# A decoder step on one Trainium2 core: the last projection and norm with tokens on partitions

## The chip, the cores and the metric

The kernel runs on one core of a Trainium2 chip. The metric is device time in microseconds for one execution, the median of three runs. Five engines work side by side: TensorE (PE; its weight loads stand in the trace as PEld), VectorE (DVE), ScalarE (ACT), GpSimd (POOL) and SyncE (SP), which here issues all transfers. Each engine works its own instructions in order and waits for the others through semaphores.

## The reference

One step of a two-layer decoder of width 1024 on 264 tokens: a prompt of 256 and eight sample tokens. Layer 0 mixes with a gated short convolution, layer 1 with attention (eight heads of 128). Each layer ends alike, and the end of layer 1 is what matters here:

```python
z = x1 @ w_z                                   # the last quarter of layer 1's input projection
y = (o.reshape(B, T, 1024) * silu(z)) @ w_out  # o: attention output
x = ALPHA * x1 + y                             # ALPHA = sqrt(2)
mu, var = x.mean(-1), square(x - mu).mean(-1)
out = (x - mu) * rsqrt(var + 1e-5) * g + b
```

## The kernel before

**Layout.** Everything is kept feature-major: `xf` holds the residual as 128 partitions x 8 feature blocks x 264 tokens (`N`; the last eight are the samples). A weight matrix is cut into slabs of 128 output features (8 blocks of 128 x 128); 80 slabs are worked in order. Slabs 40 to 71 are layer 1's input projection (q, k, v, z; `S` = 40), 72 to 79 its output projection.

**Precision.** A product is done as three fp32r matmuls: high part of the weight with high and low part of the activation, low part of the weight with the high part (`mm`, lines 121 to 128). The high part of a slab is a ScalarE cast (`hi`, line 114), the low part a VectorE subtraction (`lo`, line 119). A slab's weight is the stationary operand, the 264 tokens move past it. `m0h`, `m0l` and `m1h`, `m1l` are the activation pairs; the gated attention output `g` of the last projection is the pair `m0`.

**Order.** There is no loop scheduler. `at(n, phase, f)` (line 134) hangs a call on slab `n`, `begin(n)` runs the hooks of a slab in a fixed order of phases ahead of its matmuls, and each engine takes them in that order. Splits of slab n stand at slab n - 5 (`hi`) and one behind (`lo`), with exceptions (`hi_slot`, `lo_slot`). `load` (line 101) uses four raw buffers: the load of a slab is issued by SyncE once the low part of the slab four before has been taken. High and low parts have six buffers each. Cache pages (32 loads) share ten buffers of the pool `kvp`.

**Slabs 64 to 71.** For head `f`, `z_evac` (line 778) takes silu of the accumulator and multiplies by the attention output in `qh`; `g_split` (791) makes the pair. The samples' attention ends in between: `pvd` (741) at slab 67, `od_copy` (754) at 68, transposes on TensorE (`od_tr`, 758) and `os_fin` (763) at 69. Samples of the first six heads are multiplied in a batch (`g_batch`, 796); the last two go through `z_evac`. The earlier score products of the cache keys (`qk`, line 690 on, matmul at 697) use four column groups of TensorE with 16 columns of weight each.

**The last projection and norm, lines 925 to 964.** `out_slabs` (337) runs slabs 72 to 79 with 24 matmuls of 264 columns each; eight further ones subtract the mean of block 0 (`shift`, 269). Behind each slab come the residual (`evac`, 262), squares on ScalarE (282) and sums on GpSimd (289, 290). After slab 79 four short groups of matmuls sum over partitions (298), the statistics are finished (308 to 312), and mean and inverse are broadcast to all partitions by matmuls (`bcast_one`, 332), with three matmuls that only keep TensorE busy between them (933). Then come a subtraction (946), a multiplication (936) and an affine pass (941, 943) for each of eight blocks, shared between VectorE, GpSimd and ScalarE, and four stores of two blocks (964).

Of the kernel before, what the change touches and what calls it, by code (L numbers as in the profile page):

```python
# [10 lines left out]
F32 = mybir.dt.float32  # L11
# [7 lines left out]
D = 1024  # L19
# [10 lines left out]
EARLY = (40, 41, 42)  # L30
NU = 7
# [4 lines left out]
C_ST = 56  # L36
# [11 lines left out]
def build(tc, a):  # L48
# [3 lines left out]
    with ExitStack() as top:  # L52
# [200 lines left out]
        class Norm:  # L253
# [75 lines left out]
            def bcast_one(self, nm, c):  # L329
                p = att_tile(f"lnb{c}")[:, 0:N]  # L330
                for j in range(4):
                    pe.matmul(p[:, G * j:G * j + G], sel[:, j], self.st[:, G * c:G * c + G],  # L332
                              start=True, stop=True)
                t = self.t(nm)
                act.copy(t, p)
                return p, t

# [174 lines left out]
        with tc.tile_pool(name="l1", bufs=1) as p1, ExitStack() as late_pool:  # L512
# [5 lines left out]
            kh = [p1.tile([128, N], F32, name=f"k{h}") for h in range(8)]  # L518
# [255 lines left out]
            late = {"n": 0}  # L774

            g_t = {}

            def z_evac(f, acc):
                z = p1.tile([128, N], F32, tag="z", bufs=2, name="z")
                act.activation(z, acc, AF.Silu)  # L780
                if late["n"]:
                    n_ = N
                    pool.tensor_copy(qh[f][:, T:N], os_[:, f])
                else:
                    n_ = T
                    pool.tensor_copy(zs[:, f], z[:, T:N])
                gt = p2.tile([128, N], F32, tag="rp", bufs=3, name="gt")
                g_t[f] = gt[:, 0:n_]
                dve.tensor_mul(gt[:, 0:n_], z[:, 0:n_], qh[f][:, 0:n_])  # L789

            def g_split(f):
                n_ = g_t[f].shape[-1]
                act.copy(g[0][:, f, 0:n_], g_t[f])
                dve.tensor_sub(g[1][:, f, 0:n_], g_t[f], g[0].bitcast(F32)[:, f, 0:n_])

            def g_batch(nf):
                gt = p2.tile([128, 8, 8], F32, name="gtb")
                dve.tensor_mul(gt[:, 0:nf], os_[:, 0:nf], zs[:, 0:nf])
# [231 lines left out]
```

## Time and profile before

| | |
|---|---|
| median of three runs | 287.8 us (287.7 to 287.8) |
| the profiled execution | 287.21 us |
| its span in the trace | 285.4 us |
| TensorE busy | 275.6 us, 97% |
| VectorE, ScalarE, GpSimd busy | 186.7, 160.2, 81.5 us |
| first matmul of slab 72 | 249.03 us |
| start of the last projection matmul | 273.06 us |

Times in the trace count from the span's start. A line number with an L names the line of the kernel that made the instruction. Matmuls are pipelined: a row's duration includes its way through the array, so the distance between two starts tells what one costs. A merged row (x3) covers several instructions from the first start to the last end. In the chain that ended last, each step starts where the one that released it ended.

### The profile page before, as it was taken

To read this page: it belongs to the slowest core of one execution; us is meant where nothing else is said; L and a number is where in the kernel's file an instruction comes from. 1 tells how busy PE (TensorE), PEld (TensorE's weight loads), DVE (VectorE), ACT (ScalarE), POOL (GpSimd) and SP (SyncE) were. 2 spreads that over 40 slices of the span, in tenths; PEclk is the share of its full clock that TensorE was granted. 3 is DMA by queue.
4 is the path that set the end of the run, shared out by engine and by line. 5 is a ranking of instruction groups with operands and counts; after the bars stand their busy time and mean duration, and the time that the engine had idled before them with its cause. 6 is when DMAs were issued, how large, how long until landed. Compare 5 with 4: busy or idle time off the path is not lost.

```text
span 285.4 us, 6265 instructions
## 1 busy us (share of the span) xinstructions
PE 275.6 (97%) x2345; PEld 261.8 (92%) x2345; DVE 186.7 (65%) x350; ACT 160.2 (56%) x307; POOL 81.5 (29%) x151
## 2 busy tenths in 40 slices
PE   8999999999999999999999999999999999999980
PEld 4999999999999999999979997999869969999960
DVE  2978866556758758858997683888545355646144
ACT  4876554445556546544976683568638634562123
POOL 3222322021010106919631087201100001206643
PEclk9999999999999999999999999999999999999995
DMA  7986889999675764413039998988929972410004
GB/s 225 412 286 212 258 293 333 379 369 370 232 255 182 254 230 152 148 46 106 0 119 293 408 398 311 351 294 282 297 79 294 376 271 76 153 69 1 2 0 153
DMA packets 22640, 64.02 MB, mean 224 GB/s; under 512 B 2770, under 2 KB 5202, under 8 KB 22610
## 3 DMA queue, kind: packets, MB, share of 16 engines
q1 hardware_dynamic: 22610, 63.63, 63.9%
q8 instruction: 18, 0.29, 0.4%
q14 instruction: 12, 0.10, 0.1%
HBM read 60.30 MB, written 3.32 MB: 223 GB/s over the span
## 4 chain that ended last, share of the span: by engine, by line
PE 94%; DMA 2%; DVE 1%; ACT 1%; SPq 0%; issue 0%; DVEq 0%; ACTq 0%
PE acc L126 26%; PE acc L128 26%; PE acc L127 26%; PE sd L697 3%; PE dps L749 3%; DMA first<-first 2%; PE acc L451 1%; PE s L630 1%; PE o L669 1%; PE acc L452 1%; PE acc L455 1%; PE pt L660 1%; PE s L629 1%; DVE xf L936 1%; PE lnb L332 1%; PE o L670 1%
## 5 line engine op out<-in xcount | busy, mean ns | idle before, releaser
L119 DVE TENSOR_TENSOR lo<-raw,hi 128x1024 fp32r<-128x1024 f32 x76 | 94.3, 1250 | 5.1 <-ACT hi L114 4.9
L114 ACT CAST hi<-raw 128x1024 fp32r<-128x1024 f32 x76 | 79.2, 1049 | 32.8 <-DMA raw<-w 18.9
L128 PE MATMUL acc<-m0h,lo 128*128 128x264 f32 (+1 forms) x344 | 97.5, 283 | 0.0
L126 PE MATMUL acc<-m0h,hi 128*128 128x264 f32 (+1 forms) x344 | 97.4, 283 | 0.0
L127 PE MATMUL acc<-m0l,hi 128*128 128x264 f32 (+1 forms) x344 | 97.4, 283 | 0.0
L126 PE MATMUL acc<-m1h,hi 128*128 128x264 f32 x264 | 76.7, 290 | 0.0
L128 PE MATMUL acc<-m1h,lo 128*128 128x264 f32 x264 | 74.8, 283 | 0.0
L127 PE MATMUL acc<-m1l,hi 128*128 128x264 f32 x264 | 74.6, 283 | 0.0
L128 PEld LDWEIGHTS acc<-m0h,lo 128*128 128x128 f32 x344 | 64.9, 189 | 0.0
L126 PEld LDWEIGHTS acc<-m0h,hi 128*128 128x128 f32 x344 | 64.8, 188 | 0.1
L127 PEld LDWEIGHTS acc<-m0l,hi 128*128 128x128 f32 x344 | 64.7, 188 | 0.0
L126 PEld LDWEIGHTS acc<-m1h,hi 128*128 128x128 f32 x264 | 49.7, 188 | 1.7 <-issue 1.7
L127 PEld LDWEIGHTS acc<-m1l,hi 128*128 128x128 f32 x264 | 49.7, 188 | 0.1
L128 PEld LDWEIGHTS acc<-m1h,lo 128*128 128x128 f32 x264 | 49.7, 188 | 0.0
L407 POOL COPY uo<-up 128x10 f32<-128x10 f32 x8 | 9.0, 1126 | 65.6 <-DVE up L406 59.5
L282 ACT ACTIVATE sqm<-xf 128x264 f32<-128x264 f32 x14 | 5.8, 422 | 20.1 <-DVE xf L262 20.1
L262 DVE SCALAR_TENSOR_TENSOR xf<-xf,acc 128x264 f32<-128x264 f32 x16 | 6.6, 424 | 12.5 <-PE acc L269 10.6
L638 DVE TENSOR_TENSOR s<-s,cst 128x256 f32<-128x256 f32 x8 | 3.4, 430 | 15.5 <-PE s L630 15.5
L290 POOL TENSOR_TENSOR q<-q,sqm 128x264 f32<-128x264 f32 x12 | 13.1, 1089 | 1.6 <-ACT sqm L282 1.5
L789 DVE TENSOR_TENSOR gt<-z,q 128x256 f32<-128x256 f32 (+1 forms) x8 | 3.4, 428 | 13.0 <-ACT z L780 13.0
L609 POOL COPY vs<-vh 128x8 f32<-128x8 f32 x8 | 1.6, 204 | 35.0 <-ACT vh L608 35.0
L289 POOL TENSOR_TENSOR sr<-sr,xf 128x264 f32<-128x264 f32 x10 | 9.3, 928 | 2.3 <-DVE xf L262 2.3
(176 smaller groups left out, 358.6 us busy)
## 6 DMA issues: line engine op xcount, KB each, us to landing
raw<-w SPq DMA_DIRECT2D x76, 512.0 KB, 4.6
kv<-kc SPq DMA_DIRECT2D x32, 256.0 KB, 5.9
kv<-vc SPq DMA_DIRECT2D x16, 512.0 KB, 5.7
first<-first SPq DMA_DIRECT2D x7, 388.0 KB, 6.3
k_o<-k SPq DMA_DIRECT2D x8, 132.0 KB, 5.1
v_o<-vh SPq DMA_DIRECT2D x8, 132.0 KB, 4.2
y_o<-xf SPq DMA_DIRECT2D x4, 264.0 KB, 2.6
cst<-cst SPq DMA_DIRECT2D x1, 392.0 KB, 6.3
```

The costliest lines, as they stand in the source:

```text
L114: act.copy(his[n][sl], raws[n][sl])
L119: dve.tensor_sub(los[n][sl], raws[n][sl], his[n].bitcast(F32)[sl])
L126: pe.matmul(acc, wh, mh[:, k, 0:w], start=first and k == ks[0], stop=False)
L127: pe.matmul(acc, wh, ml[:, k, 0:w], start=False, stop=False)
L128: pe.matmul(acc, wl, mh[:, k, 0:w], start=False, stop=last and k == ks[-1])
L262: dve.scalar_tensor_tensor(x, x, ALPHA, acc, ALU.mult, ALU.add)
L282: act.activation(self.last_sq, xf[:, m], AF.Square)
L289: pool.tensor_tensor(self.sr, self.sr, xf[:, m], ALU.add)
L290: pool.tensor_tensor(self.q, self.q, self.last_sq, ALU.add)
L407: pool.tensor_copy(uo[:, f], up[:, T:N + 2])
L697: pe.matmul(s[32 * j:32 * j + 16, 0:256], zq[:, o:o + 16], kt, start=step == 0 and i == 0, stop=step == 3 and i == 3)
L749: pe.matmul(dps[0][32 * j:32 * j + 32, 512 * c:512 * c + 512], pm[b2][pg][:, j, :], kv_tiles[step, j][:, 512 * c:512 * c + 512], start=ste ...
```

## The change

The last projection turns its operands round. Columns of the gated activation (128 tokens) become the stationary operand and the output weight moves, 512 or 256 columns at a time, so that the result has tokens on partitions and features along the row; the norm is then taken along the row by VectorE's statistics instruction, with no matmul and no broadcast.

- The weight of slabs 72 to 79 is stored by rows instead of by output blocks; slab 72 + k is input block k, with all 1024 outputs. Tokens 0 to 127 come first, over all eight slabs, then the samples, then tokens 128 to 255 in pieces of 512, 256 and 256 columns. The first half still runs through `begin`, so the hooks of slabs 72 to 79 now fall between its steps.
- `x1` has to be turned as well. VectorE transposes 32 x 32 blocks of `xf` into `kall` (the former key tiles, now one tile) at slabs 65 to 67; 16 transfers at slabs 68 to 71 move the blocks back into `xf` with tokens on partitions. The order of the outputs that results (`turned`) is put into the weight, the gains and biases, and taken back by the host.
- The samples leave the fp32r path: `gs` is multiplied in fp32 with the raw weight, eight tokens padded to 32, on four column groups; four small transfers bring the result from four groups of partitions into rows.
- Gains and biases are loaded as 2 x 128 x 1024 values (`gb_load`, slab 73). Raw slabs 76 to 79 and the parts of 78 and 79 live in the cache pool.
- Of tokens 128 to 255, columns 0 to 191 are finished by ScalarE and GpSimd (`other_way`), the rest by VectorE; three stores end the kernel.

The diff, cut:

```diff
+LATE = (78, 79)
...
+        def acc_full():
+            return psp.tile([128, 512], F32, tag="acc", bufs=3, name="acc")
         def acc_tile():
-            return psp.tile([128, 512], F32, tag="acc", bufs=3, name="acc")[:, 0:N + 2]
+            return acc_full()[:, 0:N + 2]
...
         def load(n):
-            raws[n] = wp.tile([128, 8, 128], F32, tag="raw", bufs=4, name=f"raw{n}")
+            if n < 76:
+                raws[n] = wp.tile([128, 8, 128], F32, tag="raw", bufs=4, name=f"raw{n}")
+            else:
+                raws[n] = kvp.tile([128, 1024], F32, tag="kv", name=f"raw{n}").rearrange("p (a b) -> p a b", b=128)
             if n >= 4:
                 sp.dma_start(raws[n], a["w"][n - 4])
         def part(n, c):
             if n in EARLY:
                 return ex.tile([128, 8, 128], F32R, name=f"{c}{n}")
+            if n in LATE:
+                return kvp.tile([128, 1024], F32R, tag="kv", name=f"{c}{n}").rearrange("p (a b) -> p a b", b=128)
             return wp.tile([128, 8, 128], F32R, tag=c, bufs=6, name=f"{c}{n}")
...
-            kh = [p1.tile([128, N], F32, name=f"k{h}") for h in range(8)]
+            kall = p1.tile([128, 8 * N], F32, name="kall")
+            kh = [kall[:, N * h:N * h + N] for h in range(8)]
...
             def z_evac(f, acc):
                 z = p1.tile([128, N], F32, tag="z", bufs=2, name="z")
                 act.activation(z, acc, AF.Silu)
-                if late["n"]:
-                    n_ = N
...
-                g_t[f] = gt[:, 0:n_]
-                dve.tensor_mul(gt[:, 0:n_], z[:, 0:n_], qh[f][:, 0:n_])
+                pool.tensor_copy(zs[:, f], z[:, T:N])
+                gt = g_t[f] = p2.tile([128, N], F32, tag="rp", bufs=3, name="gt")[:, 0:T]
+                dve.tensor_mul(gt, z[:, 0:T], qh[f][:, 0:T])
             def g_split(f):
-                n_ = g_t[f].shape[-1]
-                act.copy(g[0][:, f, 0:n_], g_t[f])
...
-                dve.tensor_sub(g[1][:, 0:nf, T:N], gt[:, 0:nf], g[0].bitcast(F32)[:, 0:nf, T:N])
-                late["n"] = nf
+                act.copy(g[0][:, f, 0:T], g_t[f])
+                dve.tensor_sub(g[1][:, f, 0:T], g_t[f], g[0].bitcast(F32)[:, f, 0:T])
+            def sample_g():
+                dve.tensor_mul(gs[:, :, 0:8], os_, zs)
...
+            turned = kall[:, 0:2048].rearrange("p (c m q) -> p c m q", c=8, m=8)
+            xsb = xst = so = gs = x8 = None
+            xt = xf.rearrange("p m n -> p (m n)")[:, 0:2048]
+            def kv_tile(nm):
+                return kvp.tile([128, 1024], F32, tag="kv", name=nm)
+            def turn(m):
+                dve.transpose(turned[:, :, m, :], xf[:, m, 0:T].rearrange("p (c q) -> p c q", q=32))
+            def turn_move(i):
+                src = kall[32 * i:32 * i + 32, 0:2048].rearrange("p (h j f) -> p h j f", h=2, j=4)
+                for j in range(4):
+                    sp.dma_start(xt[32 * j:32 * j + 32].rearrange("p (h f) -> p h f", h=2)
+                                 [:, :, 256 * i:256 * i + 256], src[:, :, j])
+            gb = [kall[:, 1024 * i:1024 * i + 1024] for i in range(2)]
+            def gb_load():
+                for i in range(2):
+                    sp.dma_start(gb[i], a["gb"][i])
+            def sample_room():
+                nonlocal xsb, xst, so, gs, x8
+                sx = kv_tile("sx")
+                xsb, xst, so, gs = (sx[:, 256 * i:256 * i + 256] for i in range(4))
+                gs = gs.rearrange("p (k c) -> p k c", c=32)
+                x8 = kv_tile("x8")[0:8]
+                pool.memset(sx, 0.0)
+            def sample_x():
+                pool.tensor_copy(xsb.rearrange("p (m q) -> p m q", q=32)[:, :, 0:8], xf[:, :, T:N])
+            def sample_turn():
+                dve.transpose(xst, xsb)
+            class Rows:
+                def __init__(self, x, nm):
+                    self.x = x
+                    self.n = x.shape[0]
+                    self.s = lnp.tile([128, 32], F32, name=nm)[0:self.n]
+                def evac(self, c0, c1, acc):
+                    x = self.x[:, c0:c1]
+                    dve.scalar_tensor_tensor(x, x, ALPHA, acc, ALU.mult, ALU.add)
+                def stats(self, i, c0, c1):
+                    dve.bn_stats(self.s[:, 6 * i:6 * i + 6], self.x[:, c0:c1])
+                def spread(self, ns):
+                    dve.bn_aggr(self.s[:, 24:26], self.s[:, 0:6 * ns])
+                    act.activation(self.s[:, 26:27], self.s[:, 25:26], AF.Sqrt, bias=epst[0:self.n])
+                def inverse(self):
+                    dve.reciprocal(self.s[:, 27:28], self.s[:, 26:27])
+                def one(self, c0, c1):
+                    x = self.x[:, c0:c1]
+                    dve.scalar_tensor_tensor(x, x, self.s[:, 24:25], gb[0][0:self.n, c0:c1],
+                                           ALU.subtract, ALU.mult)
+                def two(self, c0, c1):
+                    x = self.x[:, c0:c1]
+                    dve.scalar_tensor_tensor(x, x, self.s[:, 27:28], gb[1][0:self.n, c0:c1],
+                                           ALU.mult, ALU.add)
+                def other_way(self, c0, c1):
+                    x, st = self.x[:, c0:c1], self.s
+                    dve.scalar_tensor_tensor(st[:, 28:29], st[:, 24:25], -1.0, st[:, 27:28], ALU.mult, ALU.mult)
+                    act.activation(x, x, AF.Identity, bias=st[:, 28:29], scale=st[:, 27:28])
+                    pool.tensor_tensor(x, x, gb[0][0:self.n, c0:c1], ALU.mult)
+                    pool.tensor_tensor(x, x, gb[1][0:self.n, c0:c1], ALU.add)
+            def wide(d, k):
+                return d[72 + k].rearrange("p a b -> p (a b)")
+            def om(acc, k, c, c0, c1):
+                t = np.s_[128 * c:128 * c + 128]
+                for i, (m, d) in enumerate(((0, his), (1, his), (0, los))):
+                    pe.matmul(acc, g[m][:, k, t], wide(d, k)[:, c0:c1],
+                              start=k == 0 and i == 0, stop=k == 7 and i == 2)
+            at(S + 26, "s1", sample_room)
+            at(S + 26, "s1", sample_x)
+            at(S + 28, "s1", sample_turn)
+            for m in range(8):
+                at(S + 25 + m // 3, "s1", turn, m)
+            for i in range(4):
+                at(S + 28 + i, "dma", turn_move, i)
+            at(S + 33, "s1", sample_g)
+            at(S + 33, "s1", table, AF.Sqrt)
+            at(S + 33, "dma", gb_load)
             ac2 = [acc_tile() for _ in range(2)]
             begin(40)
...
                     at(n + 1, "s0", z_evac, h, acc)
                     at(n + 1, "s1", g_split, h)
-            ln = Norm(1)
-            at(S + 33, "s1", table, AF.Sqrt)
...
-            for m0, m1 in ((0, 2), (2, 4), (4, 6), (6, 8)):
-                sp.dma_start(a["y_o"][:, m0:m1], xf[:, m0:m1])
+            rows = [Rows(t, f"row{i}") for i, t in enumerate([xt[:, 0:1024], xt[:, 1024:2048], x8])]
+            ac = big_tile("c0")
+            ac = [ac[:, 512 * i:512 * i + 512] for i in range(2)]
+            for k in range(8):
+                begin(72 + k)
+                for h in range(2):
+                    om(ac[h], k, 0, 512 * h, 512 * h + 512)
+            r = rows[0]
+            for h in range(2):
+                r.evac(512 * h, 512 * h + 512, ac[h])
+            for h in range(2):
+                r.stats(h, 512 * h, 512 * h + 512)
+            r.spread(2)
+            r.one(0, 512)
+            r.inverse()
+            r.other_way(512, 1024)
+            ps = att_tile("so")[:, 0:256]
+            for k in range(8):
+                for j in range(4):
+                    pe.matmul(ps[32 * j:32 * j + 32], gs[:, k, :], wide(raws, k)[:, 256 * j:256 * j + 256],
+                              start=k == 0, stop=k == 7)
+            dve.scalar_tensor_tensor(so, xst, ALPHA, ps, ALU.mult, ALU.add)
+            r.two(0, 512)
+            for j in range(4):
+                (sp if j < 2 else act).dma_start(x8[:, 256 * j:256 * j + 256], so[32 * j:32 * j + 8])
+            sp.dma_start(a["y_o"][0:128], r.x)
+            last = [acc_full(), att_tile("c1b"), att_tile("c1c")]
+            for acc, c0, c1 in zip(last, (0, 512, 768), (512, 768, 1024)):
+                for k in range(8):
+                    om(acc[:, 0:c1 - c0], k, 1, c0, c1)
+            parts = list(zip(last, (0, 512, 768), (512, 768, 1024)))
+            def part_in(i):
+                acc, c0, c1 = parts[i]
+                rows[1].evac(c0, c1, acc[:, 0:c1 - c0])
+                rows[1].stats(i, c0, c1)
+            r = rows[2]
+            for h in range(2):
+                r.stats(h, 512 * h, 512 * h + 512)
+            r.spread(2)
+            part_in(0)
+            r.inverse()
+            r.one(0, 1024)
+            part_in(1)
+            r.two(0, 1024)
+            sp.dma_start(a["y_o"][256:264], r.x)
+            part_in(2)
+            r = rows[1]
+            r.spread(3)
+            c = 192
+            r.one(c, 512)
+            r.inverse()
+            r.other_way(0, c)
+            r.two(c, 512)
+            r.one(512, 1024)
+            r.two(512, 1024)
+            for c0, c1 in ((c, 512), (0, c), (512, 1024)):
+                sp.dma_start(a["y_o"][128:256, c0:c1], r.x[:, c0:c1])
...
+    turned = np.arange(D).reshape(8, 4, 32).transpose(1, 0, 2).reshape(-1)
...
-                        slabs(np.asarray(w_in_attn)[0]), slabs(np.asarray(w_out_attn)[0])], 0)
+                        slabs(np.asarray(w_in_attn)[0]),
+                        np.asarray(w_out_attn)[0][:, turned].reshape(NB, 128, NB, 128)], 0)
...
+    gb = np.broadcast_to(np.concatenate([lg[1][turned], lb[1][turned]]), (128, 2 * D)).reshape(128, 2, D).transpose(1, 0, 2)
...
-    outs = {"y_o": (128, NB, N), "cs_o": (128, 8, 10), "st_o": (128, 64),
+    outs = {"y_o": (N, D), "cs_o": (128, 8, 10), "st_o": (128, 64),
```

## Rows read from the trace of the kernel before

**Rows 1.** The page, part 1: busy us, share of the span, instructions.

```profile
PE 275.6 (97%) x2345; PEld 261.8 (92%) x2345; DVE 186.7 (65%) x350; ACT 160.2 (56%) x307; POOL 81.5 (29%) x151
```

**Rows 2.** Chain that ended last, in order of time: start us, us, what.

```profile
273.38 0.44 DVE xf L262
...
275.73 0.75 PE warmq L933 x3
...
277.77 1.46 DVE xf L936 x4
```

**Rows 3.** Timeline of TensorE, the last projection: start us, us, line, out<-in.

```profile
249.03 0.28 PE L126 MATMUL acc<-m0h,hi 128*128 128x264 f32 x1
...
273.06 0.28 PE L269 MATMUL acc<-s,ones 128*128 128x264 f32 x1
```

**Rows 4.** Stretches: length; busy PE, PEld, DVE, ACT, POOL; granted clock; DMA share; GB/s.

```profile
224.10:227.10 3.00, 3.00 (x27) 3.00 (x26) 1.93 (x3) 1.47 (x3) 0.45 (x1) 1.00 1.01 396
...
230.00:236.70 6.70, 6.70 (x59) 4.05 (x58) 2.59 (x4) 2.22 (x4) 0.45 (x1) 1.00 0.57 190
...
249.20:261.20 12.00, 12.00 (x101) 12.00 (x101) 6.42 (x10) 6.54 (x11) 2.09 (x2) 1.00 0.12 46
```

**Rows 5.** Timeline of TensorE at the idle-filling matmuls, up to two and three.

```profile
275.54 0.71 PE L933 MATMUL warmq<-hi 128*128 128x512 f32 x2
...
275.54 0.94 PE L933 MATMUL warmq<-hi 128*128 128x512 f32 x3
```

**Rows 6.** Timeline of TensorE at a block of cache scores (line 697).

```profile
146.42 0.28 PE L128 MATMUL acc<-m1h,lo 128*128 128x264 f32 x1
146.63 3.65 PE L697 MATMUL sd<-kv,zq 128*16 128x256 f32 x64
150.20 0.39 PE L126 MATMUL acc<-m1h,hi 128*128 128x264 f32 x1
```

**Rows 7.** Groups by line, VectorE, ScalarE, GpSimd: busy us, mean ns; idle before.

```profile
L262 DVE SCALAR_TENSOR_TENSOR xf<-xf,acc 128x264 f32<-128x264 f32 x16 | 6.6, 424 | 12.5 <-PE acc L269 10.6 <-PE acc L128 1.8
...
L415 DVE SCALAR_TENSOR_TENSOR t<-up,cst,t 128x256 f32<-128x256 f32 x8 | 3.9, 482 | 8.2 <-ACT t L414 8.2
...
L640 DVE TENSOR_REDUCE mx<-s 128x1 f32<-128x256 f32 x8 | 3.3, 412 | 0.0
...
L584 DVE STREAM_SHUFFLE rsh<-rp 128x264 f32<-128x264 f32 x4 | 1.8, 452 | 0.0
...
L599 DVE SCALAR_TENSOR_TENSOR qs<-qsr,cst,qs 32x32 f32<-32x32 f32 x2 | 0.5, 240 | 0.1
...
L721 DVE RECIPROCAL dst<-dst 128x1 f32<-128x1 f32 x1 | 0.2, 164 | 0.6 <-ACT pd L717 0.6
...
L114 ACT CAST hi<-raw 128x1024 fp32r<-128x1024 f32 x76 | 79.2, 1049 | 32.8 <-DMA raw<-w 18.9 <-PE acc L127 12.2 <-PE acc L128 1.6
...
L941 ACT ACTIVATE xf<-xf,cst 128x264 f32<-128x264 f32 x5 | 2.6, 596 | 0.5 <-DVE xf L936 0.5
...
L936 POOL TENSOR_TENSOR xf<-xf,r 128x264 f32<-128x264 f32 x3 | 2.2, 757 | 0.0
```

**Rows 8.** Timeline of VectorE and GpSimd: a split alone, two beside GpSimd.

```profile
125.11 1.23 DVE L119 TENSOR_TENSOR lo<-raw,hi 128x1024 fp32r<-128x1024 f32 x1 [0.45 <-ACT hi L114]
...
259.29 3.35 DVE L119 TENSOR_TENSOR lo<-raw,hi 128x1024 fp32r<-128x1024 f32 x2
...
259.82 1.73 POOL L290 TENSOR_TENSOR q<-q,sqm 128x264 f32<-128x264 f32 x1
```

**Rows 9.** SyncE's waits for slabs 67 to 71; landings at lines 602, 964; last issue.

```profile
SPq L104 <- DVE lo L119: 20.3, 6, 6.2
...
DMA to landing us min/median/max: 3.8/5.1/8.3
...
DMA to landing us min/median/max: 2.4/2.6/2.8
...
281.63 0.42 SPq L964 DMA_DIRECT2D y_o<-xf  x1
```

More of the change, by code (lines that the diff above doesn't have):

```diff
@@ L35 @@
 C_W = 0
-C_ST = 56
+C_ST = 40
 C_ID = C_ST + 128
@@ L327, in bcast @@
                 return t
[L329 to L336, printed above, removed]
             def gcol(self, m):
@@ L772, in os_fin @@
                                    tt[:, h].rearrange("p (j c) -> p j c", c=2))
-            late = {"n": 0}
             g_t = {}
@@ L923, in build @@
                     at(n + 1, "s1", g_split, h)
-            ln = Norm(1)
-            at(S + 33, "s1", table, AF.Sqrt)
-            out_slabs(ln, 72, g, lambda m, slot: None)
-            ln.stats_mm()
-            ln.stats()
-            nd, nds = ln.bcast_one("n", 0)
-            wt = big_tile("warmq")
-            for _ in range(3):
-                pe.matmul(wt[:, 0:512], his[79][:, 0, :], his[79][:, 0:4, :], start=True, stop=True)
-            rs, rss = ln.bcast_one("r", 1)
-            def scale(e, m, r):
-                e.tensor_tensor(xf[:, m], xf[:, m], r, ALU.mult)
@@ L938, in affine @@
-            def affine(m, on_act):
-                c = xf[:, m]
-                if on_act:
-                    act.activation(c, c, AF.Identity, bias=ln.bcol(m), scale=ln.gcol(m))
-                else:
-                    dve.tensor_scalar(c, c, ln.gcol(m), ln.bcol(m), ALU.mult, ALU.add)
-            def shift(e, m, d):
-                e.tensor_tensor(xf[:, m], xf[:, m], d, ALU.add)
-            for m in (5, 6, 7):
-                shift(pool, m, nds)
-            for m in (5, 6, 7):
-                scale(pool, m, rss)
@@ L952, in build @@
-            for m in range(4):
-                shift(dve, m, nd)
-            for m in range(4):
-                scale(dve, m, rs)
-            affine(3, False)
-            shift(dve, 4, nd)
-            scale(dve, 4, rs)
-            affine(4, False)
-            affine(7, False)
-            for m in (0, 1, 5, 2, 6):
-                affine(m, True)
-            for m0, m1 in ((0, 2), (2, 4), (4, 6), (6, 8)):
-                sp.dma_start(a["y_o"][:, m0:m1], xf[:, m0:m1])
+            rows = [Rows(t, f"row{i}") for i, t in enumerate([xt[:, 0:1024], xt[:, 1024:2048], x8])]
@@ L994 @@
     cw = np.concatenate([fm(v[None])[:, :, 0] for v in
-                         (wv[0], wv[1], wv[2], lg[0], lb[0], lg[1], lb[1])], 1)
+                         (wv[0], wv[1], wv[2], lg[0], lb[0])], 1)
+    gb = np.broadcast_to(np.concatenate([lg[1][turned], lb[1][turned]]), (128, 2 * D)).reshape(128, 2, D).transpose(1, 0, 2)
     stc = np.asarray(state_conv)[0]
@@ L1001 @@
     ins = {
-        "first": first, "w": w[4:], "cst": cst,
+        "first": first, "w": w[4:], "cst": cst, "gb": gb,
         "pt": np.asarray(page_table).reshape(1, 16),
@@ L1018 @@
     r = bass_utils.run_bass_kernel_spmd(nc, [ins], core_ids=[0]).results[0]
-    y = r["y_o"].transpose(2, 1, 0).reshape(N, D)
+    y = np.empty((N, D), f32)
+    y[:, turned] = r["y_o"]
     cs = r["cs_o"].transpose(2, 1, 0).reshape(10, D)
```

11 lines of the change are left out of this document (removed).

## The prediction

> **What bounds the kernel now.** I read the page's busy line first: TensorE is busy 97% of the span [rows 1]. So only two things can move the time: the length of TensorE's own stream, and what follows it. Next the chain that ended last: until 273.2 us it is matmuls; behind them come the last norm's statistics, two broadcasts with three idle-filling matmuls between them, and VectorE's shift, scale and affine passes [rows 2]. VectorE starts on the last accumulator at 273.38 and the span ends at 285.44: a tail of 12.06 us in which TensorE does no useful projection work. The timeline gives the stretch that the change rewrites: the last projection's first matmul (slab 72) starts at 249.03, its last at 273.06 [rows 3]: 200 matmuls (8 x 24, and 8 of the mean's shift) in 199 steps, 0.1207 us each. The granted clock is 1.00 there, 2.4 GHz [rows 4].
>
> **Part 1, TensorE's stream.** Removed: those 200 matmuls of 264 columns. Added: 48 matmuls of 512 columns for tokens 0 to 127, 32 fp32 calls for the samples, 24 of 512 and 48 of 256 columns for tokens 128 to 255. Width 512 with an fp32r weight stands three times in the trace: a third one lengthens the merged row from 0.71 to 0.94, so one costs 0.23 [rows 5]. A low end: 264 columns at one per cycle of 2.4 GHz would be 0.110, 0.011 under the 0.1207 measured; if that excess is fixed, 512 columns cost 0.224. A high end is the chain's 0.75 for three, 0.25 each [rows 2]. I take 0.23, a measured step. Width 256 by the line through 264 and 512 (0.44 ns a column): 0.117. The samples' 32 calls have an exact image: the score products of the cache keys, 64 records of 256 columns on four column groups, from 146.54 (0.12 behind the start before) to 150.20: 3.66 us [rows 6]. Sum: 48 x 0.23 = 11.04, 3.66, 24 x 0.23 = 5.52, 47 x 0.117 = 5.50, so the last matmul starts at 249.03 + 25.72 = 274.75, against 273.06: TensorE ends **1.69 later**, with 0.224 for the wide ones 1.26 later, with 0.25 3.13 later.
>
> The Trainium skill (TensorE: Matmul & The Clock Gate, Back-to-back issue gap) gives a warm step as columns over 2.4 GHz and about 2.5 ns, so 0.216 for 512 and 0.1125 for 264. The rows show 0.23 and 0.1207, so the trace disagrees; by the page's figure for 512, an estimate, the 72 wide ones would take 1.0 us less and the time would be 285.4.
>
> **Part 2, the feed of that stream.** Before, a slab was used up in 3 us; now the first half uses all eight in 11 us (one in 1.38). ScalarE's and VectorE's splits of slabs 77 to 79 still stand at slabs 72 to 75; queued as they are, the last low part is done some 7 us after slab 72 begins, by the row costs of 1.05 [rows 7] and 1.23 [rows 8] for a split, and it is needed at 7 x 1.38 = 9.7. The loads of 76 to 79 no longer wait for VectorE to free a raw buffer, where SyncE now stands 20.3 of 22 us [rows 9]; instead they stand in SyncE's queue behind 16 transfers of x1, each 0.33 to issue as the loads are: 5.3 us of issue inside those 20.3 of waiting. Added traffic is 1 MB moved and 1 MB of gains and biases. I cost all of it at nothing: the cover is SyncE's waiting time, and behind it some 2.5 us of slack in the splits.
>
> **Part 3, VectorE at slabs 65 to 67.** Eight 32 x 32 turns of 128 x 256. No such row exists; the nearest is the 128 x 264 shuffle, 0.452 [rows 7]. Low end that of a plain two-input row, 0.42; high end a whole 1024-column split, 1.23 [rows 8]. I take 0.45: 3.6 us, into stretches where VectorE is busy 1.93 of 3.00 and 2.59 of 6.70 [rows 4]. They fit; low parts of the slabs are made three slabs ahead, so nobody on TensorE waits. At 1.23 they would be 9.8 us, and the copy that the samples' turn (slab 69) needs would come late. GpSimd's clearing of the samples' room and a small copy at slab 66 fall where it is busy 0.45 of 3.00. The samples' removed pieces (batch of six, two GpSimd copies) are worth nothing on the path.
>
> **Part 4, VectorE behind the first half.** The norms of tokens 0 to 127 and of the eight samples, some 11 us of VectorE work, lie beside the samples' and second half's 14.7 us of TensorE. The order is fixed: VectorE stands at the sample statistics until the four small transfers of the samples have landed, and the second half's first accumulator is behind that. My count puts the transfers' issue at 15.5 and 15.9 us after slab 72's start; with the idle-queue landing of 2.6 [rows 9] they are there at 18.5. From there statistics 1.55, then at 20.5 the first accumulator (0.72 + 0.72), reciprocal 0.16, a pass of 1024 columns 1.33, the second accumulator 0.89, the second pass 1.33: done at 25.7. The last accumulator is ready at 26.04. Cost nothing, by 0.3 us. The waits that this adds have little behind them: ScalarE issues two of the small transfers and then has only square roots and the last product; SyncE issues the other two, then waits for GpSimd's last piece of tokens 0 to 127, then for the samples' rows, and behind those stand only the last three outputs.
>
> **Part 5, the new tail.** From VectorE's start on the last accumulator, at 274.75 + 0.32 (the distance from 273.06 to 273.38) = 275.07. Durations from [rows 7], with 0.03 between dependent ones: evacuation of 256 columns 0.42; statistics 0.41 (as the reduce of 256; not shown before, from 0.35 to twice that); aggregation 0.16 (as the one-column reciprocal); first pass of 320 columns 0.55 (0.482 at 256, 0.24 at 32: 1.1 ns a column), ScalarE's square root beside it; reciprocal 0.16; a one-column product 0.2: ScalarE may start at 2.04, and its 192 columns take 0.53. GpSimd's two products of 192 columns (0.757 at 264, so 0.55 each) want to begin at 2.57. VectorE meanwhile has its second pass of 320 columns until 2.5, then two passes of 512, 0.77 each.
>
> Now what decides: a VectorE operation with two SBUF inputs and a GpSimd one don't run together. In the before two splits that take 1.23 alone took 3.35 together, beside a GpSimd row of 1.73, which otherwise takes 0.757 [rows 7, 8]: each side stood while the other worked. So: VectorE 512 until 3.2, GpSimd until 3.75, VectorE until 4.5, GpSimd until 5.05. SyncE's queue is in order: the piece of 192 columns waits for GpSimd, and the last 512 columns stand behind it, issued at about 5.5. Before, the last issue at 281.63 stood 3.8 from the span's end [rows 9], with 528 KB going out at once; here 352 KB, so I estimate 3.5. **Tail 9.0** against 12.06. The Trainium skill (SBUF — State Buffer, Who interferes with whom) states the same as an exclusive lock on a shared port pair; by that rule sharing the end between VectorE and GpSimd gives little, and the trace agrees with the 3.35.
>
> **Sum.** 275.07 + 9.0 = 284.07, against 285.44: 1.37 less. The profiled execution was 287.21, so 285.84; the median of the runs is 0.59 above it, which gives **286.4**.
>
> **Rivals.**
> 1. *No queueing at the end.* If the product-and-subtract form leaves GpSimd alone, VectorE ends at 3.95 and GpSimd at 3.65; the last issue is at 4.1, the tail 7.6: 285.0. For it: the evacuation with one PSUM input never slowed (0.424 mean) [rows 7]. Against: both inputs are in SBUF here.
> 2. *The wide matmul is faster than its rows.* 512 columns at one per cycle of 2.4 GHz, with no excess, are 0.213: 72 x 0.017 = 1.2 less, and VectorE's count of part 4 moves up with it: 285.2. For: three matmuls are few. Against: 264 columns carry 0.011 of excess. The Trainium skill's page of part 1 has this rule with a small excess.
> 3. *VectorE becomes the bound of the second half.* If statistics cost twice the reduce, it comes 1.25 late to the last accumulator and 0.35 more in the tail: 288.0, no change.
> 4. *Slower: the samples' transfers hold VectorE.* It is in order, so past a landing at 19.3 each us of delay is one of the end. Over the bound against the kernel before (1.37 + 0.6 late) it decides from a landing at 21.3, 5.4 us from issue. For: the key stores took 3.8 to 8.3 [rows 9]. Against: those went out under loaded queues; at the end, outputs took 2.4 to 2.8. A landing after 6.5 us, at 22.4, would give 286.4 + 3.1 = 289.5.
> 5. *Slower: TensorE itself.* A wide matmul of 0.26 costs 72 x 0.03 = 2.2: 288.6; a stand for a late split or a late turn adds its length to that.
>
> **How the numbers follow.** Forecast 0.45, rivals 1 to 5: 0.15, 0.12, 0.13, 0.09, 0.06. Faster by over 0.2% (0.6 us, about what a measurement of this kernel can tell from no change) is the forecast and rivals 1 and 2, less a little for the forecast's own upper end: 0.69. Within 0.2%: 0.17. Slower: 0.14. The range goes from rival 1 with part of rival 2 on top, 284.3, to rival 3, 288.1; rivals 4 and 5 stay out.
>
> **What would show it.** Right: the last matmul at 274 to 275 us with steps of 0.23 in the wide ones; GpSimd's last two rows at twice their lone time, and the last issue behind them; no gap on TensorE at slabs 72 to 79 or at the samples' turn. Wrong: an issue by SyncE before GpSimd ends, VectorE's wait for the samples' rows outlasting the second half's first accumulator, turns over 1 us, or statistics over 0.6 for 256 columns.

## The result, and the profile after

| | before | after |
|---|---|---|
| median | 287.7 us (287.25 to 287.8, 5 runs) | 285.6 us (285.36 to 286.31, 5 runs) |
| ratio, 95% interval | | 0.9932 (0.9917 to 0.9948) |
| span of the profiled execution | 285.44 us | 283.45 us |
| last projection's first matmul to its last | 24.03 us | 26.04 us |
| last matmul's start to the span's end | 12.38 us | 8.46 us |
| first matmul of the last projection to the span's end | 36.41 us | 34.50 us |

The change made the kernel 0.7% faster, 2.1 us; forecast were 1.4 us, 286.4. What TensorE lost in the last projection (2.0 us) came back twice in what follows it (3.9 us): the last store is issued 3.3 us sooner behind the last matmul (5.30 for 8.57), and the span ends 0.65 sooner behind that issue (3.16 for 3.81).

The page of the changed kernel, part 1, for the line of [rows 1]: TensorE's busy share is still 97%, VectorE's has gone from 65 to 69%.

```profile
PE 273.8 (97%) x2278; PEld 255.6 (90%) x2278; DVE 194.2 (69%) x363; ACT 155.1 (55%) x292; POOL 70.5 (25%) x139
```

Timeline of TensorE: the first and the last matmul of the last projection, for [rows 3].

```profile
248.95 0.39 PE L939 MATMUL c<-hi,m0h 128*128 128x512 f32 x1
...
274.99 0.28 PE L939 MATMUL c1c<-lo,m0h 128*128 128x256 f32 x1
```

The chain that ended last, from slab 72 on (start us, us, what), for [rows 2].

```profile
249.11 11.13 PE c L939 x48
260.25 3.59 PE so L1029 x64
263.84 5.77 PE acc L939 x24
269.60 2.83 PE c1b L939 x24
272.44 2.85 PE c1c L939 x24
...
275.31 0.43 DVE xf L903
...
277.35 0.56 ACT xf L929
...
277.98 0.91 POOL xf L930
...
278.93 0.95 POOLq L1125
```

The stages stand in it one behind another: 48 wide matmuls for tokens 0 to 127, the samples' 64 records (two for each of 32 calls), 24 wide ones and twice 24 of 256 columns for tokens 128 to 255. Behind them the statistics broadcasts and the idle-filling matmuls of [rows 2] are gone. The end now runs from VectorE through ScalarE (L929) to GpSimd: L930, and then L931, during which the chain shows GpSimd's queue (POOLq). The last two stores stood behind it: of SyncE's waits, the one on line L1069 for GpSimd's L931 was 1.7 us.

One caution for reading these traces against each other: executions of one kernel differ by up to 1 us ahead of the last projection. In a second profile of the changed kernel that first matmul started at 249.94, not 248.95. From it to the span's end it was 34.48 there and 34.50 here. The experiments are therefore compared by this distance, and by their medians beside it.

What the distance leaves out is the time of an execution that lies outside its span, that is before the first and behind the last traced instruction. It is not the same in all kernels: 1.72 to 1.85 us in the runs of the kernel before that were made beside the experiments, 2.11 to 2.20 in the ten of the changed kernel (with spans known to 0.1 us). So nearly 0.4 us of what the change wins inside the span is lost outside it.

### The profile page after: what moved, and what is told of

The parts are those of the page before. It is cut to its first block, busy times and chain, and to the rows that moved or that the text cites. A ratio compares the mean times of both kernels' runs of the same rounds, so it can differ in the third digit from the quotient of the medians.

```text
span 283.4 us, 6139 instructions
## 1 busy us (share of the span) xinstructions
PE 273.8 (97%) x2278; PEld 255.6 (90%) x2278; DVE 194.2 (69%) x363; ACT 155.1 (55%) x292; POOL 70.5 (25%) x139
## 4 chain that ended last, share of the span: by engine, by line
PE 95%; DMA 2%; DVE 1%; ACT 1%; POOLq 0%; POOL 0%; SPq 0%; issue 0%
PE acc L135 23%; PE acc L137 23%; PE acc L136 23%; PE c L939 4%; PE sd L698 3%; PE dps L750 3%; PE acc L939 2%; DMA first<-first 2%; PE acc L451 1%; PE so L1029 1%; PE s L631 1%; PE o L670 1%; PE acc L452 1%; PE acc L455 1%; PE c1c L939 1%; PE c1b L939 1%
## 5 line engine op out<-in xcount | busy, mean ns | idle before, releaser
L137 PE MATMUL acc<-m0h,lo 128*128 128x264 f32 (+1 forms) x280 | 79.4, 284 | 0.0
L136 PE MATMUL acc<-m0l,hi 128*128 128x264 f32 (+1 forms) x280 | 79.3, 283 | 0.0
L135 PE MATMUL acc<-m0h,hi 128*128 128x264 f32 (+1 forms) x280 | 79.3, 283 | 0.0
L137 PEld LDWEIGHTS acc<-m0h,lo 128*128 128x128 f32 x280 | 52.8, 189 | 0.0
L135 PEld LDWEIGHTS acc<-m0h,hi 128*128 128x128 f32 x280 | 52.7, 188 | 0.1
L136 PEld LDWEIGHTS acc<-m0l,hi 128*128 128x128 f32 x280 | 52.7, 188 | 0.0
L782 DVE TENSOR_TENSOR gt<-z,q 128x256 f32<-128x256 f32 x8 | 3.4, 425 | 11.5 <-ACT z L779 11.4
L451 PE MATMUL acc<-m0h,hi 128*128 128x264 f32 x32 | 9.1, 310 | 0.7 <-ACT hi L206 0.7
L780 POOL COPY zs<-z 128x8 f32<-128x8 f32 x8 | 3.6, 446 | 24.7 <-ACT z L779 24.7
L648 ACT ACTIVATE P<-s,mx 128x128 f32<-128x128 f32 (+1 forms) x16 | 6.6, 417 | 5.6 <-DVE mx L642 5.6
```

Source lines behind the costliest of these rows:

```text
L135: pe.matmul(acc, wh, mh[:, k, 0:w], start=first and k == ks[0], stop=False)
L136: pe.matmul(acc, wh, ml[:, k, 0:w], start=False, stop=False)
L137: pe.matmul(acc, wl, mh[:, k, 0:w], start=False, stop=last and k == ks[-1])
L451: pe.matmul(accs[s], wh, mh, start=k == 0, stop=False)
L648: act.activation(P[sl], s_ps[h][sl], AF.Exp, bias=mx[:, 2 + i:3 + i], scale=SCALE, accum_out=mx[:, 4 + i:5 + i])
```

## The experiments

**The changed kernel again**, as a measure for the runs that follow: no edit.

> The changed kernel unchanged, so that the others of this group are compared on the same chip: 285.6 us, ratio to the kernel before 0.993, span 283.4.

Measured: 285.87 us (285.31 to 286.6), ratio 0.9938 (0.9924 to 0.9952); distance 34.48 us.

**Is the shared end worth its price?**

```diff
-            c = 192
-            r.one(c, 512)
+            r.one(0, 512)
             r.inverse()
-            r.other_way(0, c)
-            r.two(c, 512)
+            r.two(0, 512)
             r.one(512, 1024)
             r.two(512, 1024)
-            for c0, c1 in ((c, 512), (0, c), (512, 1024)):
+            for c0, c1 in ((0, 512), (512, 1024)):
```

> The last 128 tokens are finished by VectorE alone, in two passes of 512 and two of 512 columns, with two stores; nothing is left to ScalarE and GpSimd. Theory (VectorE and GpSimd can't work at once on SBUF operands, so the share given away costs more than it saves): GpSimd's two products took 0.91 and 0.92 and VectorE's last pass 0.96 where it takes 0.75; without them the four passes run 276.5 to 279.5, the last store is issued at about 279.6 instead of 280.3, and the time is 0.7 to 0.9 us lower, 284.8. Rival (the share does save time): VectorE gets 192 columns twice, 0.4 us more, and nothing else moves: 286.0.

Measured: 284.81 us (284.65 to 285.37), ratio 0.9911 (0.9898 to 0.9925); distance 33.74, 0.75 less than with the share. Timeline of VectorE's passes and the last store:

```profile
278.44 0.75 DVE L917 SCALAR_TENSOR_TENSOR xf<-xf,row,kall 128x512 f32<-128x512 f32 x1
...
279.22 0.75 DVE L922 SCALAR_TENSOR_TENSOR xf<-xf,row,kall 128x512 f32<-128x512 f32 x1
...
280.00 0.33 SPq L1067 DMA_DIRECT2D y_o<-xf  x1
```

Each pass costs 0.75, none is stretched. VectorE does all 1024 columns and is done 4.25 us behind its start on the last accumulator (275.72), where in the changed kernel GpSimd is done at 4.58 and the last store follows a second one. The share cost time: the theory holds. By the medians the gain is 0.8 to 1.1; some 0.2 of it lies outside the span (1.91 to 1.97 us here).

**Do the turn of x1 and its 16 transfers cost anything?**

```diff
-            for m in range(8):
-                at(S + 25 + m // 3, "s1", turn, m)
-            for i in range(4):
-                at(S + 28 + i, "dma", turn_move, i)
```

> The eight turns of x1 on VectorE and the 16 transfers are left out (the residual of tokens 0 to 255 is then added in the wrong places; all later instructions are the same). Theory (they lie beside other work, as costed at nothing): within 0.3 us of the changed kernel, 285.6; the span of VectorE's work shrinks by 3.2 us without effect, SyncE issues slabs 76 to 79 earlier. Rival (they hold up the splits or the loads): 0.5 to 2 us lower than the changed kernel.

Measured: 285.3 us (285.05 to 285.46), ratio 0.9924 (0.9908 to 0.9939); distance 34.49. The median is 0.3 to 0.6 below the changed kernel's two, the stretch that could show a cost is the same to 0.01 us, and the last projection's first matmul stands at 249.07, no earlier than with the turn. Inside the span they lie beside other work. The median's difference lies outside it: 1.74 to 1.76 us in these runs, 2.11 to 2.20 in the changed kernel's. So the turn does cost some 0.4 us, where neither the trace nor my sum looks; whether the eight turns or the 16 transfers take it, and how, no run here shows.

**Does VectorE stand behind the samples' rows?** The four small transfers go to partitions 32 to 39 (`x9`), and one more brings the rows to their place.

```diff
-                x8 = kv_tile("x8")[0:8]
+                x8 = kv_tile("x8")
...
+            x9, x8 = x8[32:40], x8[0:8]
...
-                (sp if j < 2 else act).dma_start(x8[:, 256 * j:256 * j + 256], so[32 * j:32 * j + 8])
+                (sp if j < 2 else act).dma_start(x9[:, 256 * j:256 * j + 256], so[32 * j:32 * j + 8])
+            sp.dma_start(x8, x9)
             sp.dma_start(a["y_o"][0:128], r.x)
```

> The samples' rows go through memory twice: four small transfers to partitions 32 to 39, then one of 32 KB to partitions 0 to 7, so that they land some 2.7 us later, at about 269.8 instead of 267.1. Theory (VectorE stands at the sample statistics in its order, and 0.8 us of slack is all that covers it): statistics start 2.7 later, the second half's first accumulator 1.8 later, the last accumulator is reached at 276.2 instead of 275.3, and the time is 0.9 us higher, 286.5. Rival (the second half's matmuls set the end whatever the samples do): 285.6.

Measured: 286.55 us (286.37 to 286.77), ratio 0.997 (0.9959 to 0.9981); distance 35.37, 0.87 more. VectorE in the changed kernel, from the samples' statistics to the last thing ahead of the last accumulator:

```profile
267.14 1.38 DVE L906 BATCH_NORM_STATS2 row<-x 8x6 f32<-8x512 f32 x2 [2.08 <-DMA x<-sx]
...
269.64 0.69 DVE L903 SCALAR_TENSOR_TENSOR xf<-xf,acc 128x512 f32<-128x512 f32 x1 [0.89 <-PE acc L939]
...
272.48 0.42 DVE L903 SCALAR_TENSOR_TENSOR xf<-xf,c1b 128x256 f32<-128x256 f32 x1 [0.18 <-PE c1b L939]
...
273.27 1.26 DVE L922 SCALAR_TENSOR_TENSOR x<-x,row,kall 8x1024 f32<-8x1024 f32 x1
```

The same with the rows sent twice, and its start on the last accumulator:

```profile
270.45 1.27 DVE L906 BATCH_NORM_STATS2 row<-x 8x6 f32<-8x512 f32 x2 [5.30 <-DMA x<-x]
...
271.88 0.62 DVE L903 SCALAR_TENSOR_TENSOR xf<-xf,acc 128x512 f32<-128x512 f32 x1
...
275.18 1.26 DVE L922 SCALAR_TENSOR_TENSOR x<-x,row,kall 8x1024 f32<-8x1024 f32 x1
276.36 0.40 DVE L903 SCALAR_TENSOR_TENSOR xf<-xf,c1c 128x256 f32<-128x256 f32 x1
```

The statistics start 3.2 us later (270.45 behind a first matmul at 249.05, against 267.14 behind 248.95), and from there every VectorE row follows the one before it with no wait for TensorE. In the changed kernel VectorE was done with the samples at 274.53 and waited 0.78 for the accumulator (the row at 275.31, below among those of the end); here the accumulator waits for VectorE.

**What is late next, if TensorE is faster?**

```diff
-            for k in range(8):
+            for k in (7,):
                 for j in range(4):
                     pe.matmul(ps[32 * j:32 * j + 32], gs[:, k, :], wide(raws, k)[:, 256 * j:256 * j + 256],
-                              start=k == 0, stop=k == 7)
+                              start=True, stop=k == 7)
```

> 28 of the samples' 32 calls on TensorE are left out (one input block of eight is multiplied, so the samples' output lacks the rest). In the changed kernel the distance from the last projection's first matmul to the span's end is 34.5 us. Theory (VectorE's chain through the samples' rows is next behind TensorE): TensorE ends 3.1 us earlier, but VectorE's product of the samples stays at its place, the rows land at the same time, and the last accumulator is reached only 1.75 earlier: 32.7 us. Rival (TensorE alone sets the end): the whole 3.1: 31.4 us.

Measured: 283.91 us (282.92 to 284.58), ratio 0.9885 (0.9861 to 0.9908); distance 32.31, 2.19 less. VectorE there:

```profile
267.29 1.36 DVE L906 BATCH_NORM_STATS2 row<-x 8x6 f32<-8x512 f32 x2 [2.09 <-DMA x<-sx]
...
268.81 0.62 DVE L903 SCALAR_TENSOR_TENSOR xf<-xf,acc 128x512 f32<-128x512 f32 x1
...
271.33 0.40 DVE L903 SCALAR_TENSOR_TENSOR xf<-xf,c1b 128x256 f32<-128x256 f32 x1
...
272.11 1.25 DVE L922 SCALAR_TENSOR_TENSOR x<-x,row,kall 8x1024 f32<-8x1024 f32 x1
273.29 0.40 DVE L903 SCALAR_TENSOR_TENSOR xf<-xf,c1c 128x256 f32<-128x256 f32 x1
```

TensorE's last matmul starts 3.0 earlier (272.14 behind 249.10), VectorE's last accumulator only 2.16. The samples' rows land where they did (267.29), and from then VectorE works without a gap. The theory's place is right; its 1.75 was short. All three of VectorE's waits for TensorE in the rows of the changed kernel (0.89, 0.18 and 0.78) are gone, 1.85 together; the other 0.3 is rows that no longer wait: they start a little before the one ahead has ended, and take less (0.62 for 0.69, 0.40 for 0.42). So 0.8 of the 3.0 us can't be won back as long as the samples' rows land where they do.

**What do 192 columns cost GpSimd by themselves?** VectorE's two passes over columns 512 to 1023 are taken out.

```diff
             r.two(c, 512)
-            r.one(512, 1024)
-            r.two(512, 1024)
```

> VectorE's two passes over the last 512 columns are left out (these columns go out without the norm), so that GpSimd works alone on its 192. Theory (they exclude each other): GpSimd's two products take 0.59 each, the line through 0.757 at 264 and 1.29 at 512 columns, instead of 0.91 and 0.92, and are done 3.9 us behind VectorE's start on the last accumulator instead of 4.6. Rival (192 columns cost GpSimd 0.9 by themselves): no change in the two rows.

Measured, in one execution: 285.29 us, distance 33.83. GpSimd's two products:

```profile
278.34 0.59 POOL L930 TENSOR_TENSOR xf<-xf,kall 128x192 f32<-128x192 f32 x1 [10.27 <-ACT xf L929]
279.01 0.59 POOL L931 TENSOR_TENSOR xf<-xf,kall 128x192 f32<-128x192 f32 x1
```

0.59 each, which is on the line between 0.45 at 128 columns (in a run below) and 0.757 at 264 [rows 7], against 0.91 and 0.92 beside VectorE.

**Which VectorE work shuts GpSimd out?** ScalarE, idle there, copies gains and biases of the last 512 columns into PSUM, and VectorE's last passes read them from it. Nothing is left out.

```diff
+            gbp = big_tile("gbp")
+            gbp = [gbp[:, 512 * i:512 * i + 512] for i in range(2)]
+            for i in range(2):
+                act.copy(gbp[i], gb[i][:, 512:1024])
...
-            r.one(512, 1024)
-            r.two(512, 1024)
+            x = r.x[:, 512:1024]
+            dve.scalar_tensor_tensor(x, x, r.s[:, 24:25], gbp[0], ALU.subtract, ALU.mult)
+            dve.scalar_tensor_tensor(x, x, r.s[:, 27:28], gbp[1], ALU.mult, ALU.add)
```

> ScalarE copies gains and biases of the last 512 columns into PSUM while it is idle; VectorE's two last passes then have one operand in SBUF and one in PSUM. All work of the changed kernel is kept. Theory (only two SBUF operands shut GpSimd out): GpSimd's products 0.59 each, VectorE's passes 0.70 to 0.75 with no wait between, third store issued 4.3 us behind VectorE's start on the last accumulator instead of 5.0, and 33.9 us from the last projection's first matmul to the end instead of 34.5. Rival (any VectorE work shuts GpSimd out, or the queue between them is no lock): rows and distance as in the changed kernel.

Measured: 285.26 us (285.14 to 285.88), ratio 0.9936 (0.9922 to 0.995); distance 33.83, 0.66 less. VectorE and GpSimd at the end:

```profile
278.01 0.74 DVE L1071 SCALAR_TENSOR_TENSOR xf<-xf,row,gbp 128x512 f32<-128x512 f32 x1
...
278.29 0.59 POOL L930 TENSOR_TENSOR xf<-xf,kall 128x192 f32<-128x192 f32 x1 [10.27 <-ACT xf L929]
278.78 0.75 DVE L1072 SCALAR_TENSOR_TENSOR xf<-xf,row,gbp 128x512 f32<-128x512 f32 x1
278.96 0.59 POOL L931 TENSOR_TENSOR xf<-xf,kall 128x192 f32<-128x192 f32 x1
```

The two run side by side, each at its lone cost: 0.74 and 0.75, 0.59 and 0.59. Apart from ScalarE's two copies, which lie far ahead, only the place of the second operand has changed. That shows the mechanism that I had put the forecast on: it isn't VectorE's work that holds GpSimd up, but the second operand in SBUF of these VectorE passes. The median of these five runs doesn't show the 0.66 clearly against the changed kernel's 285.6 and 285.87; the rows and the distance do.

I overlooked that the kernel before had worked this way at its end. There VectorE's passes read the broadcast from PSUM (`lnb`):

```profile
277.77 1.45 DVE L936 TENSOR_TENSOR xf<-xf,lnb 128x264 f32<-128x264 f32 x4
278.33 2.19 POOL L936 TENSOR_TENSOR xf<-xf,r 128x264 f32<-128x264 f32 x3
279.25 0.67 DVE L943 TENSOR_SCALAR xf<-xf,cst 128x264 f32<-128x264 f32 x1
280.76 0.74 DVE L943 TENSOR_SCALAR xf<-xf,cst 128x264 f32<-128x264 f32 x2
```

Four VectorE passes in 1.45 and GpSimd's three products at 0.74 to 0.79 each: neither waited. But the rows also bound the finding: a `tensor_scalar`, whose only wide operand lies in SBUF, took 0.67 while GpSimd worked; once it was done (280.52), two of them took 0.74 together. So one SBUF operand is not free for every instruction; which ones, no run here tests.

**Does a smaller last store end sooner?** With the end on VectorE alone, the last pass and store in two halves; the diff is against that run.

```diff
-            r.two(512, 1024)
-            for c0, c1 in ((0, 512), (512, 1024)):
+            r.two(512, 768)
+            r.two(768, 1024)
+            for c0, c1 in ((0, 512), (512, 768), (768, 1024)):
```

> The end on VectorE alone, with the last pass and the last store cut into two halves of 256 columns. The end on VectorE alone took 33.74 us from the last projection's first matmul to the end. Theory (what is left behind the last pass is the last store's data as well as its landing): 128 KB less at some 350 GB/s is 0.37 us, against 0.07 for one more pass: 33.5 us. Rival (the landing of a store has one cost whatever its size): 33.8 us.

Measured: 284.84 us (284.57 to 285.18), ratio 0.992 (0.9906 to 0.9933); distance 33.72. The theory falls: the end stood 2.96 behind the last issue (279.79), with 256 KB 3.11 (280.00 in the run with the end on VectorE). The 0.15 won went into the second pass and the second issue.

**Room between the last two stores.** Gains in PSUM as above, and GpSimd's share 128 columns; the diff is against the run with gains in PSUM.

```diff
-            c = 192
+            c = 128
```

> Gains and biases of the last 512 columns in PSUM, and GpSimd's share cut from 192 to 128 columns. Theory (with 192, GpSimd and VectorE finish together and the last store stands 0.38 us behind the other's issue): GpSimd's products 0.45 each, done some 0.3 us ahead of VectorE, so that its store is issued before VectorE ends; the last issue 30.45 us behind the last projection's first matmul instead of 30.7, and 33.5 to 33.6 us to the end, against 33.84 with 192 columns and 33.74 with the end on VectorE alone. Rival (the end is set by what the stores write): 33.8.

Measured: 285.03 us (284.67 to 285.48), ratio 0.9922 (0.9908 to 0.9936); distance 33.57, the shortest with all work done.

```profile
278.78 0.45 POOL L931 TENSOR_TENSOR xf<-xf,kall 128x128 f32<-128x128 f32 x1
278.87 0.75 DVE L1072 SCALAR_TENSOR_TENSOR xf<-xf,row,gbp 128x512 f32<-128x512 f32 x1
...
279.64 0.42 SPq L1074 DMA_DIRECT2D y_o<-xf  x1
```

GpSimd ends at 279.23, VectorE at 279.62; GpSimd's piece is issued in between, and the last store right behind VectorE.

**The large store first.** Gains in PSUM, 192 columns, the stores' order changed; the diff is again against the run with gains in PSUM.

```diff
-            for c0, c1 in ((c, 512), (0, c), (512, 1024)):
+            for c0, c1 in ((c, 512), (512, 1024), (0, c)):
```

> Gains and biases of the last 512 columns in PSUM, GpSimd's share 192 columns, and the store of the last 512 columns issued ahead of the store of the 192. Theory (a small last store saves little, as with the last store of 256 columns, where it saved 0.15): last issue as before at 30.7 behind the last projection's first matmul, 33.7 us to the end. Rival (the data of the last store stand wholly behind its issue): 160 KB less at some 350 GB/s, 33.4.

Measured: 285.11 us (284.84 to 285.27), ratio 0.9924 (0.9908 to 0.9939); distance 33.77. The last issue is now one of 96 KB:

```profile
279.56 0.43 SPq L1074 DMA_DIRECT2D y_o<-xf  x1
```

The span ends 3.10 behind it (282.66), with 256 KB last it ended 3.15 behind. So making the last store the small one won next to nothing. That size itself doesn't matter is not shown: the 96 KB went out 0.4 us behind 256 KB, while in the changed kernel, where 96 KB were issued ahead of the 256, they landed 1.7 us after their issue, against 2.0 for the 256 KB of the run with the end on VectorE.

## Why the prediction was right, point by point

**Part 1, TensorE.** First to last start was forecast as 25.72 and took 26.04. The wide step, the number with the most weight, was 0.23 by [rows 5] and 0.232 here (11.13 for 48 in the chain); the samples 3.59 for 3.66; 256 columns 0.118 for 0.117. The 0.3 that were missing are not in the wide step. Timeline of TensorE around the samples:

```profile
259.85 0.40 PE L939 MATMUL c<-lo,m0h 128*128 128x512 f32 x1
260.18 3.66 PE L1029 MATMUL so<-raw,sx 128*32 128x256 f32 x64
263.77 0.50 PE L939 MATMUL acc<-hi,m0h 128*128 128x512 f32 x1
264.11 0.39 PE L939 MATMUL acc<-hi,m0l 128*128 128x512 f32 x1
```

The step into the fp32 samples is 0.33 and the first one behind them 0.34, where the others of both wide stages are 0.232: 0.1 more at each change between the wide fp32r matmuls and the fp32 ones on column groups. The first of the two was in my 3.66, which began one step behind the start of the matmul before (measured in the same way it is 3.69 here); the second was not. It stood in the trace of the kernel before too: behind the block of [rows 6] the first matmul takes 0.23 (150.20 to 150.43), not 0.12. So the 0.3 are 0.14 for 72 steps of 0.232 instead of 0.23, 0.03 in the samples, 0.1 behind them, and 0.05 in the 47 of 256 columns. The high end, 0.25, and rival 5's 0.26 are out. So is rival 2: the page of the Trainium skill that stood in part 1 (TensorE: Matmul & The Clock Gate, Back-to-back issue gap) would have had 0.216 for 512 columns by its formula; the changed kernel's rows show 0.232 here, too, in a stream of fp32r matmuls with a weight load for each.

**Part 2, the feed.** No wait of TensorE stands in the chain between slab 72 and the end of the first half. The last low part was done at 255.7, 6.7 us behind the first matmul (forecast 7), and 3 us ahead of that slab's first matmul at 258.7. One term was mis-sized: a transfer of x1 took not 0.33 but 0.595 to issue, and SyncE was at it from 232.8 to 246.5 us, with the loads of 76 to 79 in between. The cover, SyncE's waiting time, held all the same, but it was thinner than I said: 5.7 us of it were left of 20.3. The load of slab 79 was issued at 246.61, still 1.9 us sooner than the 248.53 of before. The turns on VectorE, SyncE's issues and its remaining wait (228 to 250 us):

```profile
L865 DVE STREAM_TRANSPOSE kall<-xf x8: 402/404/440, 225.5 to 232.4; 128x256 f32<-128x256 f32 x8
...
L870 SPq DMA_DIRECT2D xf<-kall x16: 591/595/1973, 232.8 to 245.9; - x16
...
DMA to landing us min/median/max: 2.2/3.4/3.6
...
SPq L111 <- DVE lo L128: 5.7, 2, 3.2
```

**Part 3, the turns.** 0.404 each, forecast 0.45 by the shuffle's row [rows 7]; leaving them and the transfers out changed the distance by 0.01. But I had costed the two at nothing for the whole execution, and that is wrong by the 0.4 us outside the span.

**Part 4, VectorE behind the first half.** The statistics started 18.2 us behind the first matmul (forecast landing 18.5), and the slack ahead of the last accumulator was 0.78 (forecast 0.3). Rival 4, the samples' transfers, did not come about, but its mechanism is real: with the rows sent twice they landed 21.4 behind the first matmul, and the last accumulator waited 0.96 longer for VectorE (27.31 us behind the first matmul for 26.35). So it decides from a landing at about 20.4, not at 19.3: VectorE has two more waits for TensorE to give up (0.89 and 0.18), which I had counted in part, and rows that don't wait follow each other closer.

**Part 5, the tail.** Forecast 9.0 from VectorE's start on the last accumulator; it was 8.14 (275.31 to 283.45). The rows of the end:

```profile
275.31 0.42 DVE L903 SCALAR_TENSOR_TENSOR xf<-xf,c1c 128x256 f32<-128x256 f32 x1 [0.78 <-PE c1c L939]
275.76 0.43 DVE L906 BATCH_NORM_STATS2 row<-xf 128x6 f32<-128x256 f32 x1
276.23 0.24 DVE L909 BATCH_NORM_AGGREGATE row<-row 128x2 f32<-128x18 f32 x1
...
277.70 0.75 DVE L917 SCALAR_TENSOR_TENSOR xf<-xf,row,kall 128x512 f32<-128x512 f32 x1
...
277.98 0.91 POOL L930 TENSOR_TENSOR xf<-xf,kall 128x192 f32<-128x192 f32 x1 [10.27 <-ACT xf L929]
278.48 0.96 DVE L922 SCALAR_TENSOR_TENSOR xf<-xf,row,kall 128x512 f32<-128x512 f32 x1
278.97 0.92 POOL L931 TENSOR_TENSOR xf<-xf,kall 128x192 f32<-128x192 f32 x1
...
280.29 0.42 SPq L1069 DMA_DIRECT2D y_o<-xf  x1
```

Statistics took 0.43 for the reduce's 0.41, so rival 3 is out; the aggregation 0.24 for 0.16. The step that gave most of the 0.9 is the queueing of GpSimd and VectorE, and it is a matter of size. I had let them work strictly in turn and GpSimd end at 5.05; it ended at 4.58. GpSimd's first product began 0.47 before VectorE's pass was over and needed only 0.44 more of its 0.59 behind it. The queueing costs 0.32 to 0.33 for each product and 0.21 for VectorE's last pass (0.96 for 0.75), less than turns in full. The other part is the stores: the last issue stood 3.16 from the span's end, not 3.5. Before, it was 3.8 [rows 9]; the runs above put it at 2.96 to 3.16 for a last store of 96 to 256 KB.

**The sum.** TensorE 0.3 longer, the tail 0.9 shorter than forecast: distance 34.50 instead of 35.04. The sign, the places and the order of what ends last were as forecast; rival 1, no queueing, is what the run with gains in PSUM makes: a tail of 7.48, forecast 7.6, and 0.66 better than the change. The two errors have opposite signs, so they cancel in part in the distance. The rest of the way from 286.4 to 285.6 is luck: the last projection began 0.08 sooner; to the span I had added 1.77 us outside it, as in the profiled execution before, and it was 2.15; and the 0.59 by which the median then lay above that execution did not come again. The last two cancel for the most part.

**A version that beats both.** The end on VectorE alone (284.81) and GpSimd's share of 128 columns with gains in PSUM (285.03) are 0.75 and 0.92 shorter than the changed kernel by distance. Their intervals against the kernel before, 0.9898 to 0.9925 and 0.9908 to 0.9936, overlap, so which is better stays open; the former has less code, and less time outside the span (1.91 to 1.97 us for 2.12 to 2.21), which offsets the latter's 0.17 of distance.

## What to carry to other kernels

Before work at the end is shared out between VectorE and GpSimd, look where the operands lie: two SBUF operands on VectorE make GpSimd wait and the other way round, and either one engine alone or VectorE's second operand in PSUM was faster here. When a projection's orientation is changed, sum the whole of TensorE's stream: here the eight samples, 3% of the tokens, took 14% of it, and the gain was all behind it. Compare traces from a fixed instruction inside the stretch, not from the span's start, if what stands ahead of it moves more than the effect, and look beside it at the time outside the span.

## What the runs showed of the hardware that I had not expected

- *VectorE and GpSimd.* With a gain in SBUF, GpSimd's 192 columns took 0.91, with VectorE quiet 0.59, with VectorE at work on a gain in PSUM 0.59. The Trainium skill (SBUF — State Buffer, Who interferes with whom) names the shared port pair as the one place where engines wait for each other on SBUF; the runs agree, and add that the wait was shorter than the other's whole instruction here: some 0.32 of VectorE's 0.75.
- *The time to issue a transfer.* 0.595 us for 32 partitions of 2 x 1 KB, against 0.33 for a slab's 128 rows of 4 KB in the median; issued between those transfers, a slab's load took 0.53, so how much of it is the shape is not shown. The samples' four small ones took 0.64 to 1.48 on ScalarE's and SyncE's queues.
- *The end behind the last store.* 2.96 to 3.16 us for the last store of 96 to 256 KB; a size that is halved saved 0.15.
- *Time outside the span.* 2.11 to 2.20 us in the changed kernel, 1.74 to 1.76 without its turn and 16 transfers; the cause is open.
